# x, the memory and the constant columns arrive transposed; the head splits them k tile by k tile

## The chip, the cores and the metric

The kernel runs on one core of one Trainium2 chip. The metric is the time of the whole kernel on the device in microseconds (us). TensorE, VectorE, ScalarE, GpSimd and SyncE are written PE, DVE, ACT, POOL and SP, as in the profile; PEld is PE's weight load. SP issues nearly all transfers (DMAs) here, in the order of its program. Layout work that the host does on the inputs before the launch is not part of the time.

## The reference

One block of a network on 512 tokens of 1,024 numbers: a mixer (an HGRN2 recurrence and an mLSTM, four heads each), attention to a memory of 256 rows, and a convolutional feed-forward, each with a residual and a layer norm.

```python
proj = x @ w_in + b_in                  # (512,1024) @ (1024,4104)
hq, hf, hi, hg, mq, mk, mv, mo, mi, mf = split(proj)   # 8 x 512 columns, then 4 + 4 gate columns
log_f = log(lb + (1 - lb) * sigmoid(hf))
o_hg = head_rms_norm(hgrn2(silu(hq), (1 - lb) * sigmoid(-hf), hi, log_f)) * silu(hg)
qk = silu(causal_dwconv(concat(mq, mk)))
h_ml = mlstm(q_ml, k_ml, mv, mi, log_sigmoid(mf))
o_ml = sigmoid(mo) * head_layer_norm(h_ml)
x = layer_norm(ALPHA * x + concat(o_hg, o_ml) @ w_out)
x = layer_norm(ALPHA * x + cross_attention(x, mem))    # k, v = mem @ wkv
x = layer_norm(ALPHA * x + conv_ffn(x))
```

## The kernel before

Every large product is made of three matmuls: an operand is split into a rounded high part and the rest (`wh`, `wl` for weights, `xTh`, `xTl` for x), and `mm3` (lines 155 to 158) adds high x high, high x low and low x high into one PSUM bank. The high part is an ACT copy, the low part a DVE subtraction: `split` (line 119) for weights, `split_evict` (line 244) for what comes out of PSUM. Weights come in pieces of 1 MB into three buffers called `raw` (`load_raw`, line 111), which are free again when both parts are made. `slab_units` loads 4 k tiles of 512 columns, `col_units` 8 k tiles of 256 columns; a k tile is 128 of the 1,024 numbers that a product sums over.

The head of the program (lines 92 to 108 and 261 to 303) makes the projection `HI`. x is loaded in four blocks of 128 tokens; `transpose_block` (line 249) turns each on PE (8 transposes of 128x128 into two banks, line 254) and splits it, and the matmuls of a block (`hi_mm`) follow as transposed blocks and weights are there. PE, ACT and DVE run in the written order in this part. Elsewhere the order on each engine is set by a scheduler from its own estimate of times, not by the source alone.

Behind the head, eight small DMAs fetch biases and convolution weights as rows (lines 308 to 316), three transposes and a DVE copy turn them into `cols`, one constant per partition and column (lines 322 to 326), and eight tiny operations make the bound `lb` of the forget gate. Two further loads (`hnw`, `mnw`) and the eight gate columns (`wif`) follow.

The gates of the mLSTM come next: 16 matmuls of `wif` with x (lines 362, 363), then a serial chain on DVE and ACT (lines 368 to 399: `z`, `e`, `bl`, `ae`, ...), and four small PE transposes of its result (line 404). In PE's order these four stand behind 78 matmuls of the projection `HF`, whose weights are the first two 1 MB pieces loaded with `col_units` (columns 0 to 255 and 256 to 511 of `HF`). In DVE's order the first operation of the gate chain (`z`, line 368) stands behind the low part of the second of these pieces (line 126).

Much later, between the mLSTM's convolutions and its heads, the memory is transposed by 16 PE transposes (line 581) into four banks and split into `mTh`, `mTl`.

Of the kernel before, what the change touches and what calls it, by code (L numbers as in the profile page):

```python
# [37 lines left out]
def hybrid_block_kernel(  # L38
    ctx: ExitStack,
    tc: tile.TileContext,  # L40
    x: bass.AP,
    mem: bass.AP,
    w_in: bass.AP,
    b_in: bass.AP,
    hg_lb_logits: bass.AP,
    hg_norm_w: bass.AP,
    ml_conv_w: bass.AP,
    ml_conv_b: bass.AP,
    ml_norm_w: bass.AP,
# [8 lines left out]
    ffn_w_up: bass.AP,  # L58
    ffn_conv_w: bass.AP,
    ffn_conv_b: bass.AP,  # L60
    ffn_w_down: bass.AP,
# [39 lines left out]
    w_in0 = w_in[0]  # L101
    xin = [X8(F32, "xin") for _ in range(2)]
    xblk = [xin[b // 2][:, (b % 2) * D:(b % 2 + 1) * D] for b in range(NB)]
    raw0 = wp.tile([P, 2048], F32, name="raw", tag="raw", bufs=3).rearrange("p (a c) -> p a c", a=4)
    for b in range(NB):
        nc.sync.dma_start(xblk[b], x[0, b * P:(b + 1) * P, :])
        if b < 2:
            nc.sync.dma_start(raw0[:, 2 * b:2 * b + 2, :], w_in0[2 * b * P:2 * (b + 1) * P, HI:HI + 512]
                              .rearrange("(k p) c -> p k c", p=P))

    def load_raw(src_list, shape):
        r = wp.tile([P, 2048], F32, name="raw", tag="raw", bufs=3)
# [15 lines left out]

    def slab_units(w, c0, nk, raw=None):

        k, per = 0, (2 if raw is not None else 4)
        while k < nk:
            n = min(4, nk - k)
            if k or raw is None:
                raw = load_raw(
                    lambda rv, k=k, n=n: [(rv[:, j:min(j + per, n), :],
                                           w[(k + j) * P:(k + min(j + per, n)) * P, c0:c0 + 512]
                                           .rearrange("(k p) c -> p k c", p=P)) for j in range(0, n, per)],
                    (4, 512))
# [20 lines left out]
    def slab(xh, xl, w, c0, nk, evict, blocks=NB, late=0, raw=None, mid=None, mid_k=4, halves=False):  # L160

# [14 lines left out]

        for u in slab_units(w, c0, nk, raw):
# [83 lines left out]
    def kslice(ts_, k, c0=0, n=S):  # L261
        o = (k % 4) * 512 + c0
        return ts_[k // 4][:, o:o + n]
# [13 lines left out]

    def hi_mm(b, u):
        k0, n, h, l = u
        for i in range(n):  # L280
            k = k0 + i
            mm3(ps[b], kslice(xTh, k, b * P, P), kslice(xTl, k, b * P, P), h[:, i, :], l[:, i, :],
                k == 0, k == KT - 1)

    units = slab_units(w_in0, HI, KT, raw0)
    with tc.manual_schedule(engines={mybir.EngineType.PE, mybir.EngineType.Activation, mybir.EngineType.DVE}):
        us = []
        tb = lambda b, **kw: transpose_block(xblk[b], b, xTh, xTl, **kw)
        tb(0, mid=lambda: us.append(next(units)))
        tb(1)  # L290
        hi_mm(0, us[0])
        us.append(next(units))
        hi_mm(1, us[0])
        tb(2)
        hi_mm(0, us[1])
        tb(3)
        hi_mm(1, us[1])
        for b in (2, 3):
            hi_mm(b, us[0])
            hi_mm(b, us[1])  # L300
        for u in units:
# [6 lines left out]
    rows = q1p.tile([P, 3, P], F32, name="rows")  # L308
    r2 = lambda ap: ap.rearrange("(r c) -> r c", c=P)
    nc.sync.dma_start(rows[0:32, 0, :], r2(b_in[0, 0:4096]))  # L310
    nc.sync.dma_start(rows[32:64, 0, :], ml_conv_w[0].rearrange("j (r c) -> (j r) c", c=P))
    nc.sync.dma_start(rows[64:72, 0, :], r2(ml_conv_b[0]))
    nc.sync.dma_start(rows[72:80, 0, :], hg_lb_logits.rearrange("j (r c) -> (j r) c", c=P))
    for j in range(4):
        src = ffn_conv_w[0, j] if j < 3 else ffn_conv_b[0]
        nc.sync.dma_start(rows[44 * (j % 2):44 * (j % 2) + 44, 1 + j // 2, :], r2(src))
# [5 lines left out]
    ps = mx_bank()  # L322
# [545 lines left out]
    def ln3_evict(b, ps, cs):  # L868
# [10 lines left out]

_INS = ['x', 'mem', 'w_in', 'b_in', 'hg_lb_logits', 'hg_norm_w', 'ml_conv_w', 'ml_conv_b', 'ml_norm_w',  # L880
        'w_out', 'ln1_g', 'ln1_b', 'ca_wq', 'ca_wkv', 'ca_wo', 'ln2_g', 'ln2_b',
        'ffn_w_up', 'ffn_conv_w', 'ffn_conv_b', 'ffn_w_down', 'ln3_g', 'ln3_b']

# [10 lines left out]


# [7 lines left out]
```

## Time and profile before

| | us |
|---|---|
| time, median of 3 runs | 829.31 |
| lowest and highest of the 3 | 828.69, 829.79 |
| time of the profiled execution | 829.24 |
| its span, first to last instruction | 827.5 |
| PE busy in the span | 809.6 |
| PE waits for another engine or a DMA, the five longest | 4.3, 2.4, 1.6, 1.1, 0.6 |

The span is 1.74 us shorter than the time of the same execution. Times in the rows are counted from the start of the span. In the chain of waits a row is a start, a length and what it was; "issue" is time in which nothing that the profile shows was waited for. In the table of stretches the columns are the stretch, its length, the busy time of five engines with the number of instructions, PE's granted clock as a share of full speed, the share of the 16 DMA engines that was busy, and GB/s.

### The profile page before, as it was taken

The page shows a single profiled execution, that of the slowest core. Times are in us where ns is not written, and L with a number is a line of the kernel's source. Part 1 is how long each engine was busy: PE and PEld are TensorE (multiplying, and loading weights), DVE is VectorE, ACT ScalarE, POOL GpSimd, SP SyncE. Part 2 cuts the span into 40 slices and gives each one's busy share as a digit, 9 for nine tenths or more (in the row PEclk, how much of TensorE's full clock was granted, in tenths as well). Part 3 has the DMA queues.
Part 4 walks back from the last instruction along what each step waited for, and adds up shares of the span by engine and source line. Part 5 has one row for each costly group of instructions (what it writes and reads, how often), then busy time and mean ns, then how long its engine had stood idle before and what let it go on. Part 6 is the DMA issues. An engine that isn't in the chain of part 4 may idle for free.

```text
span 827.5 us, 10149 instructions
## 1 busy us (share of the span) xinstructions
PE 809.6 (98%) x4051; PEld 682.2 (82%) x4051; DVE 504.4 (61%) x863; ACT 323.1 (39%) x443; POOL 31.6 (4%) x52
## 2 busy tenths in 40 slices
PE   8979999999999999999999999999999999999996
PEld 7868877778779888889988988888888888888885
DVE  4374378888878289338638685566665666224237
ACT  4169653344235215226512364444444444221110
POOL 1000100010120000000001000000000000000001
PEclk9999999999999999999999999999999999999998
DMA  7845534034426613431311533333333322242102
GB/s 250 188 93 134 133 65 102 12 91 102 143 74 220 239 51 137 168 102 52 102 51 51 154 104 101 102 102 102 102 103 101 91 83 83 75 153 70 59 0 102
DMA packets 85156, 87.88 MB, mean 106 GB/s; under 512 B 3184, under 2 KB 64880, under 8 KB 85108
## 3 DMA queue, kind: packets, MB, share of 16 engines
q1 hardware_dynamic: 84524, 84.58, 34.4%
q10 hardware_dynamic: 584, 2.64, 0.8%
q8 instruction: 32, 0.52, 0.3%
q14 instruction: 16, 0.13, 0.0%
HBM read 85.10 MB, written 2.12 MB: 105 GB/s over the span
## 4 chain that ended last, share of the span: by engine, by line
PE 88%; DVE 5%; DMA 3%; POOL 1%; ACT 1%; issue 1%; SPq 0%; DVEq 0%; ACTq 0%; POOLq 0%
PE mm L156 27%; PE mm L157 27%; PE mm L158 27%; DMA raw<-in_w_in_dram 3%; PE mx L254 1%; PE mx L605 1%; PE mx L617 1%; POOL ss L451 1%; DMA xin<-in_x_dram 1%; PE mx L492 1%; PE mx L493 1%; PE mx L156 0%; PE mx L158 0%; PE mx L157 0%; PE mx L445 0%
## 5 line engine op out<-in xcount | busy, mean ns | idle before, releaser
L126 DVE TENSOR_TENSOR wl<-raw,wh 128x1024 fp32r<-128x1024 f32 x138 | 168.1, 1223 | 233.1 <-ACT wh L125 232.1
L125 ACT CAST wh<-raw 128x1024 fp32r<-128x1024 f32 x138 | 145.2, 1055 | 247.9 <-PE mm L158 135.1
L156 PE MATMUL mm<-x2h,wh 128*128 128x512 f32 (+1 forms) x384 | 142.8, 372 | 0.0
L157 PE MATMUL mm<-x2l,wh 128*128 128x512 f32 (+1 forms) x384 | 142.6, 371 | 0.0
L158 PE MATMUL mm<-x2h,wl 128*128 128x512 f32 (+1 forms) x384 | 142.6, 371 | 0.0
L158 PEld LDWEIGHTS mm<-x2h,wl 128*128 128x128 f32 x384 | 72.4, 188 | 12.6
L157 PEld LDWEIGHTS mm<-x2l,wh 128*128 128x128 f32 x384 | 72.4, 188 | 12.5
L156 PEld LDWEIGHTS mm<-x2h,wh 128*128 128x128 f32 x384 | 72.4, 188 | 12.3
L157 PE MATMUL mm<-wl,hTh 128*128 128x512 f32 (+1 forms) x198 | 72.4, 366 | 0.0
L156 PE MATMUL mm<-wh,hTh 128*128 128x512 f32 (+1 forms) x198 | 72.4, 366 | 0.0
L826 DVE SCALAR_TENSOR_TENSOR fc<-mm,cols,fc 128x511 f32<-128x511 f32 x88 | 65.7, 747 | 1.5
L158 PE MATMUL mm<-wh,hTl 128*128 128x512 f32 (+1 forms) x180 | 65.8, 365 | 0.0
L156 PE MATMUL mm<-wh,xTh 128*128 128x512 f32 x128 | 52.1, 407 | 0.0
L158 PE MATMUL mm<-wh,xTl 128*128 128x512 f32 x128 | 51.6, 403 | 0.0
L157 PE MATMUL mm<-wl,xTh 128*128 128x512 f32 x128 | 51.4, 401 | 0.0
L156 PE MATMUL mm<-xTh,wh 128*128 128x512 f32 x128 | 51.2, 400 | 0.0
L157 PE MATMUL mm<-xTl,wh 128*128 128x512 f32 x128 | 51.0, 399 | 0.0
L158 PE MATMUL mm<-xTh,wl 128*128 128x512 f32 x128 | 50.9, 397 | 0.0
L156 PEld LDWEIGHTS mm<-wh,hTh 128*128 128x128 f32 x198 | 37.4, 189 | 6.1
L157 PEld LDWEIGHTS mm<-wl,hTh 128*128 128x128 f32 x198 | 37.4, 189 | 6.1
L158 PEld LDWEIGHTS mm<-wh,hTl 128*128 128x128 f32 x180 | 33.9, 189 | 5.5
L835 ACT CAST hTh<-fc 128x512 fp32r<-128x512 f32 x22 | 13.7, 622 | 55.8 <-DVE fc L834 55.8
(274 smaller groups left out, 1401.3 us busy)
## 6 DMA issues: line engine op xcount, KB each, us to landing
raw<-in_ffn_w_up_dram SPq DMA_DIRECT2D x44, 512.0 KB, 4.3
raw<-in_w_in_dram SPq DMA_DIRECT2D x14, 1024.0 KB, 8.1
raw<-in_ffn_w_down_dram SPq DMA_DIRECT2D x10, 1024.0 KB, 5.0
raw<-in_ca_wkv_dram SPq DMA_DIRECT2D x8, 1024.0 KB
raw<-in_w_out_dram SPq DMA_DIRECT2D x4, 1024.0 KB, 10.1
raw<-in_ca_wq_dram SPq DMA_DIRECT2D x4, 1024.0 KB, 7.2
raw<-in_ca_wo_dram SPq DMA_DIRECT2D x4, 1024.0 KB
wt<-scr ACTq DMA_DIRECT2D x4, 640.0 KB
```

The costliest lines, as they stand in the source:

```text
L125: A.copy(hv, src)
L126: V.tensor_sub(lv, src, f32(hv))
L156: T.matmul(ps, ah, bh, start=first, stop=False, skip_group_check=True)
L157: T.matmul(ps, ah, bl, start=False, stop=False, skip_group_check=True)
L158: T.matmul(ps, al, bh, start=False, stop=last, skip_group_check=True)
L254: T.transpose(ps[:, i * P:(i + 1) * P], src[:, k * P:(k + 1) * P], ident)
L451: G.tensor_tensor(out_, out_, neghalf[:, 0:n], op=OP.pow)
L492: T.matmul(at[:, s], ke[:, s], qe[:, s], start=True, stop=True, skip_group_check=True)
L493: T.matmul(at[0:CH, b * P + CH:(b + 1) * P], kxe[:, b, :], qbo[:, b, :], start=True, stop=True, skip_group_check=True)
L605: T.matmul(ps[:, 0:LEN[j]], kT_[:, j * P:(j + 1) * P], qT_[:, j * P:], start=True, stop=True)
L826: V.scalar_tensor_tensor(y[:, s:], ps[:, :S - s], col(FCW + (2 - s) * 44 + ft), y[:, s:], op0=OP.mult, op1=OP.add)
L835: A.copy(kslice(hTh, i), g)
```

## The change

The host hands over x transposed (`x_t`, 1024x512) beside x, the memory transposed (`mem_t`, 1024x256), and all constant columns as one array (`cols_in`, 128x256). The kernel drops the transposes of x, of the memory and of the constants. The head takes k tiles in five steps of 1, 1, 2, 2 and 2 (`HEAD`): each step loads its rows of the weights and of `x_t` into one `raw` buffer (two halves), makes the high part of the weights on ACT and the three other parts on DVE, and runs all four token blocks. x itself is still loaded later for the residual.

```diff
+HEAD = ((0, 1), (1, 1), (2, 2), (4, 2), (6, 2))
...
-    for b in range(NB):
-        nc.sync.dma_start(xblk[b], x[0, b * P:(b + 1) * P, :])
-        if b < 2:
-            nc.sync.dma_start(raw0[:, 2 * b:2 * b + 2, :], w_in0[2 * b * P:2 * (b + 1) * P, HI:HI + 512]
-                              .rearrange("(k p) c -> p k c", p=P))
+    xraw, raw0 = [], []
+    for j, (k0, n) in enumerate(HEAD):
+        xr = wp.tile([P, 2048], F32, name="raw", tag="raw", bufs=3)
+        xraw.append(xr.rearrange("p (a c) -> p a c", a=4))
+        raw0.append(xraw[-1][:, 2:4, :])
+        for dst, src in ((raw0[-1], w_in0[:, HI:HI + 512]), (xraw[-1], x_t)):
+            nc.sync.dma_start(dst[:, 0:n, :], src[k0 * P:(k0 + n) * P, :].rearrange("(k p) c -> p k c", p=P))
...
-        tb(0, mid=lambda: us.append(next(units)))
-        tb(1)
-        hi_mm(0, us[0])
...
+        for (k0, n), xr, wr in zip(HEAD, xraw, raw0):
+            h = wp.tile([P, 1024], F32R, name="wh", tag="wh", bufs=4).rearrange("p (a c) -> p a c", a=2)
+            l = wp.tile([P, 1024], F32R, name="wl", tag="wl", bufs=4).rearrange("p (a c) -> p a c", a=2)
+            xk = lambda ts_: ts_[k0 // 4].rearrange("p (a c) -> p a c", a=4)[:, k0 % 4:k0 % 4 + n, :]
+            A.copy(h[:, 0:n, :], wr[:, 0:n, :])
+            V.tensor_copy(xk(xTh), xr[:, 0:n, :])
+            V.tensor_sub(l[:, 0:n, :], wr[:, 0:n, :], f32(h[:, 0:n, :]))
+            V.tensor_sub(xk(xTl), xr[:, 0:n, :], f32(xk(xTh)))
             for b in range(NB):
-                hi_mm(b, u)
+                for i in range(n):
+                    k = k0 + i
+                    mm3(ps[b], kslice(xTh, k, b * P, P), kslice(xTl, k, b * P, P), h[:, i, :], l[:, i, :],
+                        k == 0, k == KT - 1)
...
-    nc.sync.dma_start(rows[0:32, 0, :], r2(b_in[0, 0:4096]))
...
-    T.transpose(ps[:, 0:80], rows[0:80, 0, :], ident[0:80, 0:80])
-    T.transpose(ps[:, 80:168], rows[0:88, 1, :], ident[0:88, 0:88])
-    T.transpose(ps[:, 168:256], rows[0:88, 2, :], ident[0:88, 0:88])
-    V.tensor_copy(cols, ps[:, 0:256])
+    nc.sync.dma_start(cols, cols_in)
...
-    memraw = load_raw(lambda rv: [(rv, mem[0].rearrange("(b p) c -> p b c", p=P))], (2, 1024))
+    memraw = load_raw(lambda rv: [(rv, mem_t.rearrange("(k p) c -> p k c", p=P))], (8, 256))
...
-                T.transpose(ps[:, i * 256 + b * P:i * 256 + (b + 1) * P], memraw[:, b, k * P:(k + 1) * P], ident)
-        s = slice(j * 512, (j + 1) * 512)
-        split_evict(ps, mTh[:, s], mTl[:, s])
+    for j in range(2):
+        s = slice(j * 4, (j + 1) * 4)
+        m8 = lambda t: t.rearrange("p (a c) -> p a c", a=8)[:, s, :]
+        A.copy(m8(mTh), memraw[:, s, :])
+        V.tensor_sub(m8(mTl), memraw[:, s, :], f32(m8(mTh)))
```

On SP, from the small loads behind the head to the first three 1 MB pieces of weights (`raw` with 128x8x256: the two of `HF` and the first of `HQ`), the order before is:

```order
L310 DMA rows<-in_b_in_dram 32x128
L311 DMA rows<-in_ml_conv_w_dram 32x128
L312 DMA rows<-in_ml_conv_b_dram 8x128
L313 DMA rows<-in_hg_lb_logits_dram 8x128
L316 DMA rows<-in_ffn_conv_w_dram 44x128 x3
L316 DMA rows<-in_ffn_conv_b_dram 44x128
L318 DMA hnw<-in_hg_norm_w_dram 128x512
L320 DMA mnw<-in_ml_norm_w_dram 128x512
L349 DMA wif<-in_w_in_dram 128x8x8
L358 DMA bif<-in_b_in_dram 4x1
L359 DMA bif<-in_b_in_dram 4x1
L116 DMA raw<-in_w_in_dram 128x8x256 x3
```

The same place on SP after the change, from the last two steps of the head on:

```order
L108 DMA raw<-in_w_in_dram 128x2x512
L108 DMA raw<-in_x_t_dram 128x2x512
L108 DMA raw<-in_w_in_dram 128x2x512
L108 DMA raw<-in_x_t_dram 128x2x512
L290 DMA binb<-in_b_in_dram 128x512
L294 DMA cols<-in_cols_in_dram 128x256
L296 DMA hnw<-in_hg_norm_w_dram 128x512
L298 DMA mnw<-in_ml_norm_w_dram 128x512
L321 DMA wif<-in_w_in_dram 128x8x8
L330 DMA bif<-in_b_in_dram 4x1
L331 DMA bif<-in_b_in_dram 4x1
L115 DMA raw<-in_w_in_dram 128x8x256 x3
```

The eight loads of rows are one load of columns, and the last pieces of the head stand where they stood. Each DMA signals on one of eight semaphores in turn, so a DMA waits for the one eight places ahead of it to land; the first piece of `HF` now waits in that way for the head's last piece of `x_t`, and for its buffer.

On DVE, from the eviction of `HI` (`hv`) to the first operation of the gate chain (`z`), before:

```order
L306 TENSOR_TENSOR hv<-mm,binb 128x512 x4
L326 COPY cols<-mx 128x256
L126 TENSOR_TENSOR wl<-raw,wh 128x1024
L329 TENSOR_SCALAR nbin<-cols 128x32
L333 TENSOR_TENSOR lbm<-cols 128x4
L335 TENSOR_TENSOR le<-cols,lbm 128x4
L336 TENSOR_TENSOR le<-cols,lbm 128x4
L339 TENSOR_TENSOR ls<-le 128x4
L341 RECIPROCAL lr<-ls 128x4
L344 TENSOR_TENSOR lb<-le,lr 128x4
L345 TENSOR_SCALAR oml<-lb 128x4
L368 TENSOR_SCALAR z<-mm,bif 4x512
```

On DVE at the same place after the change (the three `wl` are the two halves of the first piece of `HF` and the first half of the second):

```order
L313 RECIPROCAL lr<-ls 128x4
L328 TENSOR_TENSOR wh<-wif,wh 128x8x4
L316 TENSOR_TENSOR lb<-le,lr 128x4
L317 TENSOR_SCALAR oml<-lb 128x4
L125 TENSOR_TENSOR wl<-raw,wh 128x1024
L292 TENSOR_TENSOR hv<-mm,binb 128x512 x2
L125 TENSOR_TENSOR wl<-raw,wh 128x1024
L292 TENSOR_TENSOR hv<-mm,binb 128x512 x2
L125 TENSOR_TENSOR wl<-raw,wh 128x1024
L340 TENSOR_SCALAR z<-mm,bif 4x512
```

The tiny operations on `cols` moved ahead of the weights; `z` still stands behind the first half of the second piece of `HF`.

On PE, at the end of the last `mq` tile, before:

```order
L156 MATMUL mm<-xTh,wh 128x512
L157 MATMUL mm<-xTl,wh 128x512
L158 MATMUL mm<-xTh,wl 128x512
L581 MATMUL mm<-ident,raw 128x128 x16
L605 MATMUL mx<-u 128x512
```

and after:

```order
L154 MATMUL mm<-xTh,wh 128x512
L155 MATMUL mm<-xTl,wh 128x512
L156 MATMUL mm<-xTh,wl 128x512
L574 MATMUL mx<-u 128x512
L574 MATMUL mx<-u 128x384
```

The 16 transposes are gone and the mLSTM's first product follows at once. The ACT copies and DVE subtractions of the memory moved up, among the convolutions of the `mk` tiles.

## Rows read from the trace of the kernel before

**Rows 1.** Busy time of the engines, first part of the page.
```profile
PE 809.6 (98%) x4051; PEld 682.2 (82%) x4051; DVE 504.4 (61%) x863; ACT 323.1 (39%) x443; POOL 31.6 (4%) x52
```
**Rows 2.** What PE waited for: us in total, times, longest.
```profile
PE mx L404 <- ACT ae L399: 4.3, 1, 4.3
PE mx L445 <- DVE y L534: 2.4, 3, 1.1
PE mx L254 <- DMA xin<-in_x_dram: 1.6, 1, 1.6
```
**Rows 3.** Chain that ended last, 14 to 62 us: start, length, what.
```profile
18.76 20.91 DMA raw<-in_w_in_dram
...
39.77 1.06 ACT wh L125
...
40.86 1.23 DVE wl L126
...
43.60 0.76 DVE z L368
...
60.77 0.64 ACT ae L399
...
61.45 0.43 PE mx L404 x4
```
**Rows 4.** Timeline of PE: start, length, instruction [idle before].
```profile
35.54 0.48 PE L362 MATMUL mm<-xTh,wh 128*128 128x512 f32 x1
...
39.26 0.39 PE L156 MATMUL mm<-xTh,wh 128*128 128x512 f32 x1
...
56.72 0.39 PE L158 MATMUL mm<-xTh,wl 128*128 128x512 f32 x1
...
62.41 0.63 PE L157 MATMUL mm<-xTl,wh 128*128 128x512 f32 x1
...
65.31 0.40 PE L158 MATMUL mm<-xTh,wl 128*128 128x512 f32 x1
```
**Rows 5.** Table of stretches.
```profile
4.00:6.00 2.00, 1.95 (x10) 1.68 (x9) 0.00 (x0) 0.35 (x1) 0.00 (x0) 1.00 1.02 242
7.00:9.00 2.00, 0.92 (x5) 0.95 (x6) 1.38 (x2) 1.08 (x2) 0.00 (x0) 1.00 1.07 391
24.00:28.00 4.00, 4.00 (x19) 3.31 (x18) 0.32 (x2) 0.34 (x2) 0.29 (x1) 1.00 0.97 165
60.00:65.00 5.00, 3.55 (x12) 2.83 (x13) 1.21 (x3) 4.96 (x7) 0.00 (x0) 0.68 0.01 1
207.00:213.00 6.00, 6.00 (x29) 4.96 (x28) 6.00 (x11) 1.44 (x3) 0.00 (x0) 1.00 0.98 341
```
**Rows 6.** Chain that ended last, 0 to 20 us.
```profile
8.08 1.94 PE mx L254 x8
10.02 0.43 PE mm L156
...
14.22 0.23 PE mm L157
```
**Rows 7.** Timeline of SP: when DMAs were issued.
```profile
6.54 0.35 SPq L310 DMA_DIRECT2D rows<-in_b_in_dram  x1
...
15.70 0.29 SPq L316 DMA_DIRECT2D rows<-in_ffn_conv_b_dram  x1
...
18.25 6.03 SPq L116 DMA_DIRECT2D raw<-in_w_in_dram  x3
```
**Rows 8.** Timeline of ACT: the first piece of HF is there.
```profile
32.38 1.05 ACT L125 CAST wh<-raw 128x1024 fp32r<-128x1024 f32 x1 [7.71 <-DMA raw<-in_w_in_dram]
```
**Rows 9.** DVE's groups of instructions: count | busy, mean ns | idle before.
```profile
L246 DVE TENSOR_TENSOR xTl<-mx,xTh 128x512 fp32r<-128x512 f32 x8 | 5.3, 689 | 9.0 <-ACT xTh L245 9.0
L416 DVE TENSOR_SCALAR kin<-kin,oml 128x512 f32<-128x512 f32 x4 | 1.9, 480 | 3.1 <-ACT kin L415 3.1
```
**Rows 10.** Timeline of PE: the transposes of the memory.
```profile
203.74 1.91 PE L581 MATMUL mm<-ident,raw 128*128 128x128 f32 x16
```

More of the change, by code (lines that the diff above doesn't have):

```diff
@@ L41, in hybrid_block_kernel @@
     x: bass.AP,
-    mem: bass.AP,
+    x_t: bass.AP,
+    mem_t: bass.AP,
+    cols_in: bass.AP,
     w_in: bass.AP,
     b_in: bass.AP,
-    hg_lb_logits: bass.AP,
     hg_norm_w: bass.AP,
-    ml_conv_w: bass.AP,
-    ml_conv_b: bass.AP,
     ml_norm_w: bass.AP,
@@ L101, in hybrid_block_kernel @@
     w_in0 = w_in[0]
-    xin = [X8(F32, "xin") for _ in range(2)]
-    xblk = [xin[b // 2][:, (b % 2) * D:(b % 2 + 1) * D] for b in range(NB)]
-    raw0 = wp.tile([P, 2048], F32, name="raw", tag="raw", bufs=3).rearrange("p (a c) -> p a c", a=4)
-    for b in range(NB):
-        nc.sync.dma_start(xblk[b], x[0, b * P:(b + 1) * P, :])
-        if b < 2:
-            nc.sync.dma_start(raw0[:, 2 * b:2 * b + 2, :], w_in0[2 * b * P:2 * (b + 1) * P, HI:HI + 512]
-                              .rearrange("(k p) c -> p k c", p=P))
+    xraw, raw0 = [], []
[5 more added lines that the diff above has]
+            nc.sync.dma_start(dst[:, 0:n, :], src[k0 * P:(k0 + n) * P, :].rearrange("(k p) c -> p k c", p=P))
     def load_raw(src_list, shape):
@@ L127, in split, with slab_units @@
         return hv, lv
-    def slab_units(w, c0, nk, raw=None):
-        k, per = 0, (2 if raw is not None else 4)
+    def slab_units(w, c0, nk):
+        k, per = 0, 4
         while k < nk:
             n = min(4, nk - k)
[L134 to L139, printed above, removed]
+            raw = load_raw(
+                lambda rv, k=k, n=n: [(rv[:, j:min(j + per, n), :],
+                                       w[(k + j) * P:(k + min(j + per, n)) * P, c0:c0 + 512]
+                                       .rearrange("(k p) c -> p k c", p=P)) for j in range(0, n, per)],
+                (4, 512))
             for u in range(0, n, 2):
@@ L158, in mm3, with slab @@
         T.matmul(ps, al, bh, start=False, stop=last, skip_group_check=True)
-    def slab(xh, xl, w, c0, nk, evict, blocks=NB, late=0, raw=None, mid=None, mid_k=4, halves=False):
+    def slab(xh, xl, w, c0, nk, evict, blocks=NB, late=0, mid=None, mid_k=4, halves=False):
         ps = [mm_bank() for _ in range(blocks)]
@@ L175, in run @@
                     mm3(pb, xh(k, b), xl(k, b), h[:, i, cs], l[:, i, cs], k == 0, k == nk - 1)
-        for u in slab_units(w, c0, nk, raw):
+        for u in slab_units(w, c0, nk):
             k0, n, h, l = u
@@ L276, in hybrid_block_kernel @@
     ps = [mm_bank() for _ in range(NB)]
[L278 to L285, printed above, removed]
-    with tc.manual_schedule(engines={mybir.EngineType.PE, mybir.EngineType.Activation, mybir.EngineType.DVE}):
-        us = []
-        tb = lambda b, **kw: transpose_block(xblk[b], b, xTh, xTl, **kw)
-        tb(0, mid=lambda: us.append(next(units)))
-        tb(1)
-        hi_mm(0, us[0])
[L292 to L301, printed above, removed]
+    with tc.manual_schedule(engines={mybir.EngineType.PE, mybir.EngineType.Activation, mybir.EngineType.DVE}):
+        for (k0, n), xr, wr in zip(HEAD, xraw, raw0):
[6 more added lines that the diff above has]
+            V.tensor_sub(xk(xTl), xr[:, 0:n, :], f32(xk(xTh)))
             for b in range(NB):
-                hi_mm(b, u)
+                for i in range(n):
+                    k = k0 + i
+                    mm3(ps[b], kslice(xTh, k, b * P, P), kslice(xTl, k, b * P, P), h[:, i, :], l[:, i, :],
+                        k == 0, k == KT - 1)
     nc.sync.dma_start(binb, bcast(b_in[0, HI:HI + 512], 512))
@@ L306, in hybrid_block_kernel @@
         V.tensor_add(hv[:, b, :], ps[b], binb)
-    rows = q1p.tile([P, 3, P], F32, name="rows")
-    r2 = lambda ap: ap.rearrange("(r c) -> r c", c=P)
-    nc.sync.dma_start(rows[0:32, 0, :], r2(b_in[0, 0:4096]))
[L311 to L316, printed above, removed]
+    nc.sync.dma_start(cols, cols_in)
     hnw = q1p.tile([P, 512], F32, name="hnw")
@@ L877, in hybrid_block_kernel @@
     slab(tok(hTh), tok(hTl), ffn_w_down[0], 512, NPAIR, ln3_evict, late=4, halves=True)
-_INS = ['x', 'mem', 'w_in', 'b_in', 'hg_lb_logits', 'hg_norm_w', 'ml_conv_w', 'ml_conv_b', 'ml_norm_w',
+_INS = ['x', 'x_t', 'mem_t', 'cols_in', 'w_in', 'b_in', 'hg_norm_w', 'ml_norm_w',
         'w_out', 'ln1_g', 'ln1_b', 'ca_wq', 'ca_wkv', 'ca_wo', 'ln2_g', 'ln2_b',
-        'ffn_w_up', 'ffn_conv_w', 'ffn_conv_b', 'ffn_w_down', 'ln3_g', 'ln3_b']
+        'ffn_w_up', 'ffn_w_down', 'ln3_g', 'ln3_b']
 def build(shapes):
@@ L893, in build, with laid_out @@
     return nc
+def laid_out(inputs):
+    a = {n: np.asarray(v) for n, v in inputs.items()}
+    a["x_t"], a["mem_t"] = a["x"][0].T, a["mem"][0].T
+    rows = [a["b_in"][0, 0:4096], a["ml_conv_w"], a["ml_conv_b"], a["hg_lb_logits"],
+            a["ffn_conv_w"], a["ffn_conv_b"]]
+    a["cols_in"] = np.concatenate([r.reshape(-1, P) for r in rows]).T
+    return {n: np.ascontiguousarray(a[n]) for n in _INS}
 def kernel(**inputs):
     from concourse.bass_utils import run_bass_kernel_spmd as _run
-    arrays = {f"in_{n}_dram": np.ascontiguousarray(inputs[n]) for n in _INS}
+    arrays = {f"in_{n}_dram": v for n, v in laid_out(inputs).items()}
     nc = build({n: arrays[f"in_{n}_dram"].shape for n in _INS})
```

8 lines of the change are left out of this document (removed).

## The prediction

> **What bounds the kernel now.** I read the busy times first: PE is busy for 809.6 us of 827.5, so nearly everything that shortens PE's stream or one of its waits counts in full, and what the other engines save counts only where PE waits for them [rows 1]. The list of PE's waits comes next. The longest is a single one of 4.3 us: the four gate transposes (line 404) wait for the last ACT step of the gate chain (line 399). The first transposes of x wait 1.6 us for their data [rows 2].
>
> The chain of waits tells why the 4.3 us are there. The weights of the second piece of `HF` land at 39.67 (18.76 + 20.91). ACT copies (1.06), DVE subtracts (1.23), and eight tiny operations follow until `z` starts at 43.60; the gate chain runs to 61.41, and PE goes on at 61.45 [rows 3]. So from `z` to PE's restart it is 17.85 us. PE itself had begun the gate matmuls at 35.54 and the 78 matmuls of `HF` at 39.26, 0.227 us apart (77 steps to 56.72), and was through them at about 57.0 [rows 4]. The late end is that of the gate chain, and its start hangs on a transfer, not on PE.
>
> The wait has a second price. From 60 to 65 us the granted clock is 0.68 on average [rows 5], and single matmuls last 0.63 where they last 0.40 from 65.31 on [rows 4]: after standing still, PE runs at 1.2 GHz and then again at 2.4. Some 8 matmuls at 0.43 apart instead of 0.227 are 1.65 us. In the head the chain's pieces show the same two levels: 0.43 per matmul from 10.02, 0.23 from 14.22, about 6 us after PE has begun to work without a pause at 8.08 [rows 6].
>
> **The head.** The 32 transposes of x go. What is left on PE up to the gate matmuls is 96 matmuls. Before, the first two transfers (1 MB) had landed when SP went on at 6.54 [rows 7], and half of that, one block of x, allowed the first transposes at about 4.5. The new first step needs the same half megabyte (weights and x of one k tile), so its data are there at about 4.5. A DVE cast of 512 columns from SBUF has no row; the nearest are 0.480 for a scalar operation and 0.689 for a subtraction [rows 9], I take 0.5. First matmul at 5.0; the second and third each wait for one more DVE subtraction, so PE works without a pause from about 6.3, not from 8.08. If the clock rises as long after that as before, it does so at 12.2; then 15.7 matmuls are done and the other 80.3 take 18.2 us: end at 30.4. Bounds: a rise 3.9 us after the start (as from 61.45 to 65.31) gives 29.5, a rise at 14.0 as before gives 31.2. DVE does not hold this up: two k tiles cost it 1.0 + 2 x 1.22 = 3.4 us, PE 24 x 0.227 = 5.4 us. The tightest place is the third step, whose second megabyte lands at 9.2 to 10 at 391 GB/s [rows 5] and is split by 12.6 to 13.4; PE comes there at 14.1.
>
> The Trainium skill (DMA: Bandwidth & Descriptors, section Bandwidth) says that DMAs should be at least 1 MiB to reach three quarters of the peak, which speaks against steps of 256 KB. Here 512 KB transfers queued one behind the other ran at 391 GB/s [rows 5]; smaller pieces in the same queue are shown by no row.
>
> The 16 gate matmuls end at 30.4 + 3.65 = 34.05, where the trace has 39.26: PE is 5.2 us ahead. It is through the 78 `HF` matmuls at 34.05 + 17.7 = 51.8, if the first piece of `HF` is split by 34 (it was there at 32.38 before [rows 8] and comes earlier, below).
>
> **The loads behind the head.** The three transposes and the copy of `cols` (0.4 us each or less) are hidden or gone; one load replaces eight. What counts is SP's order. Each of the eight had to wait for an older transfer to land, the last was issued at 15.70, and the first piece of `HF` at 18.25 [rows 7]. Now it waits for the head's last x, the same 4 MB, which before had landed shortly before 15.70: I take 15.2. That is 3.05 us sooner. The second piece needs a buffer whose last use is DVE's fourth step, at about 16.7. In front of both stand `binb` and `cols`, 384 KB or about 1.0 us at 391 GB/s. With the queue's pace unchanged the second piece lands at 39.67 - 3.05 + 1.0 = 37.6, call it 37.5.
>
> The pace is the open cost. Over 24 to 28 us the engines were 97% busy and moved 165 GB/s; later, on `ca_wkv`, 341 [rows 5]. At 165 GB/s on average the two pieces (2.1 MB) take 12.7 us; that they took longer before must be engines that lag behind the others. Begun at about 18.5, behind `hnw`, `mnw` and `wif`, and with all engines even, they land at about 32. At 341 GB/s they would be there before 27. I take the middle between 32 and 37.5, that is 34.7: there is no longer a standstill of the queue behind the head, but nothing makes these reads fast.
>
> The Trainium skill (the same page, section Latency and other measured facts) reports that rows spaced at large powers of two read slowly and that a small pad does not help; its rows are much longer than the 16,416 bytes of `w_in`. By that rule the slow reads belong to `w_in` and stay, which is the first rival's time. The trace agrees in part: `ca_wkv`, spaced at exactly 8,192 bytes, is the fast one.
>
> **The gate chain.** The eight tiny operations now stand before the weights. With the second piece at 34.7, ACT starts at 34.8, DVE's subtraction ends at 37.1, `z` starts, and PE restarts at 37.1 + 17.85 = 54.95 instead of 61.45: 6.5 us. PE then waits 3.1 us. Whether the clock falls after a pause that is a quarter shorter no row shows; I take half of the 1.65 us as gained: 0.8.
>
> **The memory.** 16 transposes last 1.91 us on PE [rows 10], 1.75 without the overlap with the next matmul. PE waits for nothing there, before or after, so 1.75 is gained. ACT's copies and DVE's subtractions (as many columns as before) move up beside the `mk` tiles. ACT now waits for the memory's load with a copy of `yTh` and two evictions of `mk` behind it; the load was on its way some 6 us before that place, so I cost the wait at nothing, and at up to 1 us if it is late.
>
> **Sum.** 6.5 + 0.8 + 1.75 = 9.05 us, from the profiled execution's 829.24 (0.07 below the median of the runs): 820.2.
>
> **Rivals.**
> First, the reads keep their pace, with the same laggards: the second piece at 37.5, `z` at 39.9, PE's restart at 57.75. 3.7 + 1.75 = 5.45, and the slow stretch stays: 823.8. For it: every first stretch of a `w_in` load is slow. Against it: the standstill before these loads is gone.
>
> Second, the reads are quick and PE is the bound: once the piece lands before about 31.5, `z` starts when the gate matmuls are done, 34.2, the chain ends at 52.05, and PE has been there since 51.8. 9.4 + 1.65 + 1.75 = 12.8: 816.4. For it: the head's reads of the same weights run at 391 GB/s when x lies between them, and now nothing stops in between.
>
> Third, slower: `w_in` is read slowly throughout. Its pieces now come first, in small steps; at the 242 GB/s of 4 to 6 us [rows 5] the head's 4.2 MB end 5.1 us later than they did, and if both pieces of `HF` take the 14.1 us that the first took from issue (18.25 to 32.38), the second lands at 15.2 + 5.1 + 28.2 = 48.5. PE restarts at 68.75: 7.3 lost, 1.75 gained, 834.8. It decides from a landing after 44.7 on. Against it: reads between x's were fast from 7 us on.
>
> That the change does little is the case between the first and third: a landing at 41 to 44.
>
> **How the numbers follow.** The forecast (820.2, on its own 817.5 to 822.5) has 0.42, the first rival 0.26, the second 0.21, the third 0.06, and 0.05 lie at no change, within 0.2% or 1.7 us, which is about what this kernel's runs can tell apart. Faster is the sum of the first three: 0.89. The range that should hold the time 8 times in 10 reaches from below the second rival's 816.4, for a clock that rises early (0.9 us) and a little more, to above the first rival's 823.8 with a longer slow stretch and 1 us lost at the memory: 814.5 to 826.5.
>
> **What would show it.** In the changed profile: PE's first matmul of `HI` near 5 us and the last gate matmul near 34; the second piece of `HF` landing near 35; `z` about 2.4 us after it; one wait of PE before the gate transposes, of 2 to 4 us, and the granted clock after it; no transposes before the mLSTM's first product. I am wrong if the second piece lands before 31 or after 37, if PE starves between the five steps of the head, or if a new wait of PE appears beside the `mk` tiles or in the mLSTM's heads, where the order changed too.

## The result and the profile after

The changed kernel takes 819.93 us (median of four runs, 819.76 to 821.82); the kernel before, run beside it, 829.49 (828.69 to 829.79). The ratio is 0.9891, interval 0.9874 to 0.9908: faster by 9.6 us. The forecast was 820.2, with 814.5 to 826.5 as the range. The profiled execution took 819.77, 9.47 less than the profiled one of before; its span is 818.1, shorter by 9.4. A second set of runs, below, gives 8.3 us (ratio 0.9898).

Busy time of the engines after the change; it answers to [rows 1]:

```profile
PE 801.5 (98%) x4000; PEld 674.0 (82%) x4000; DVE 504.9 (62%) x863; ACT 318.8 (39%) x434; POOL 30.2 (4%) x52
```

What PE waited for (us in total, times, longest); it answers to [rows 2]:

```profile
PE mx L376 <- ACT ae L371: 3.5, 1, 3.5
PE mx L417 <- DVE y L506: 2.4, 3, 1.1
PE mx L210 <- DVE warm L207: 1.1, 1, 1.1
PE mm L154 <- DVE xTh L282: 0.8, 1, 0.8
PE mm L156 <- DVE xTl L284: 0.6, 1, 0.6
PE mm L155 <- DVE wl L283: 0.5, 1, 0.5
```

The gate transposes (now line 376) are still the longest wait, still on the last ACT step of the gate chain, for 3.5 us instead of 4.3. The 1.6 us for x are gone; three shorter waits inside the head have taken their place.

The chain that ended last (start, length, what); it answers to [rows 3]:

```profile
9.26 7.34 DMA binb<-in_b_in_dram
...
16.68 17.60 DMA raw<-in_w_in_dram
...
34.39 1.06 ACT wh L124
...
36.73 0.75 DVE z L340
...
53.89 0.64 ACT ae L371
...
54.57 0.43 PE mx L376 x4
```

It has the same shape as before. The second piece of `HF` lands at 34.28 (16.68 + 17.60), ACT and DVE split its first half, `z` starts at 36.73, and 17.84 us later PE goes on, at 54.57 instead of 61.45.

PE in the head, at the gate matmuls and around the pause (start, length, what, idle time before); it answers to [rows 4]:

```profile
5.24 0.47 PE L154 MATMUL mm<-wh,xTh 128*128 128x512 f32 x1 [0.77 <-DVE xTh L282]
...
6.69 0.40 PE L154 MATMUL mm<-wh,xTh 128*128 128x512 f32 x1
6.93 0.40 PE L155 MATMUL mm<-wl,xTh 128*128 128x512 f32 x1
...
12.45 0.50 PE L155 MATMUL mm<-wl,xTh 128*128 128x512 f32 x1 [0.54 <-DVE wl L283]
13.59 0.50 PE L156 MATMUL mm<-wh,xTl 128*128 128x512 f32 x1 [0.63 <-DVE xTl L284]
...
32.99 0.39 PE L335 MATMUL mm<-xTl,wh 128*128 128x512 f32 x1
...
50.67 0.39 PE L156 MATMUL mm<-xTh,wl 128*128 128x512 f32 x1
54.57 0.43 PE L376 MATMUL mx<-ident,ae 36*128 36x36 f32 x4 [3.52 <-ACT ae L371]
...
56.25 0.63 PE L156 MATMUL mm<-xTh,wl 128*128 128x512 f32 x1
...
59.62 0.40 PE L155 MATMUL mm<-xTl,wh 128*128 128x512 f32 x1
```

Two things are to be seen. From 6.7 us on the matmuls stand 0.23 apart, the pitch of the higher level, 2.4 GHz. In the head the level can be read off the pitch alone: the granted clock in the table of stretches is 1.00 there in both kernels, also where the matmuls of before were 0.43 apart [rows 6]:

```profile
10.00:14.00 4.00, 4.00 (x11) 3.12 (x10) 2.43 (x3) 1.53 (x2) 0.00 (x0) 1.00 1.04 407
```

And after the pause of 3.5 us the clock falls all the same, 1.6 us later, for about 3.4 us (56.2 to 59.6), as long as before.

Two stretches of the table (columns as in [rows 5]):

```profile
22.00:26.00 4.00, 4.00 (x20) 3.30 (x19) 0.00 (x0) 0.00 (x0) 0.00 (x0) 1.00 0.29 95
56.00:60.00 4.00, 4.00 (x12) 3.14 (x11) 2.33 (x4) 3.56 (x5) 0.00 (x0) 0.57 0.00 0
```

While the first piece of `HF` is awaited, the DMA engines are 29% busy and move 95 GB/s, less than the 165 of before over 24 to 28 us, when they were 97% busy [rows 5]. These are two kinds of slowness. Divided by 16 engines and their busy share, it is 20.5 GB/s for a busy engine here and 10.6 there (estimates from these rows): after the change an engine is not slow while it is busy, but idle for most of the time. What the engines wait for no row shows.

SP's issue of the pieces of `HF`, DVE's first step on x in the third step of the head, and the mLSTM's first product, where the 16 transposes stood [rows 7, 9, 10]:

```profile
16.05 5.00 SPq L115 DMA_DIRECT2D raw<-in_w_in_dram  x3
```
```profile
10.57 0.69 DVE L282 CAST xTh<-raw 128x1024 fp32r<-128x1024 f32 x1 [2.30 <-DMA raw<-in_x_t_dram]
```
```profile
196.84 2.10 PE L574 MATMUL mx<-u 128*128 128x512 f32 x6
```

Where the 9.4 us of the span come from is read at four places. PE's restart: 61.45 - 54.57 = 6.88. The end of the projections, where before the transposes begin: 203.74 - 196.84 = 6.90, so nothing was won or lost in between. The mLSTM's first product: 205.48 - 196.84 = 8.64, the transposes' 1.74. The last matmul: 819.99 - 810.75 = 9.24: another 0.6 us. That is a wait of 0.6 us which before followed the mLSTM's first products and which the list of waits after the change no longer has. Before:

```profile
PE mx L605 <- DVE wt L606: 0.6, 1, 0.6
```

### The profile page after: what moved, and what is told of

Its sections match the earlier page's. It is cut to its first block, busy times and chain, and to the rows that moved or that the text cites. A ratio compares the mean times of both kernels' runs of the same rounds, so it can differ in the third digit from the quotient of the medians.

```text
span 818.1 us, 10034 instructions
## 1 busy us (share of the span) xinstructions
PE 801.5 (98%) x4000; PEld 674.0 (82%) x4000; DVE 504.9 (62%) x863; ACT 318.8 (39%) x434; POOL 30.2 (4%) x52
## 3 DMA queue, kind: packets, MB, share of 16 engines
q1 hardware_dynamic: 85632, 84.58, 33.6%
## 4 chain that ended last, share of the span: by engine, by line
PE 88%; DVE 5%; DMA 4%; POOL 1%; issue 1%; ACT 0%; SPq 0%; DVEq 0%; ACTq 0%; POOLq 0%
PE mm L154 27%; PE mm L155 27%; PE mm L156 27%; DMA raw<-in_w_in_dram 3%; PE mx L574 1%; DMA binb<-in_b_in_dram 1%; PE mx L586 1%; PE mx L252 1%; PE mx L464 1%; POOL ss L423 1%; DMA raw<-in_x_t_dram 1%; PE mx L465 1%; PE mx L154 0%; DVE wl L125 0%; PE mx L156 0%
## 5 line engine op out<-in xcount | busy, mean ns | idle before, releaser
L125 DVE TENSOR_TENSOR wl<-raw,wh 128x1024 fp32r<-128x1024 f32 x134 | 163.2, 1221 | 230.3 <-ACT wh L124 229.7
L124 ACT CAST wh<-raw 128x1024 fp32r<-128x1024 f32 x134 | 140.7, 1052 | 242.8 <-PE mm L156 133.0
```

What stands on the lines that cost most here:

```text
L124: A.copy(hv, src)
L125: V.tensor_sub(lv, src, f32(hv))
```

## The experiments

Each kernel ran beside the kernel before, whose medians in the three sessions were 829.10, 828.83 and 828.95; ratios are to those. What is read from a profile is read from one execution.

The theory: the second piece of `HF` decides when `z` starts and so when PE goes on; the head on PE matters only up to that point. Rivals: PE's own head brings the gain; or the parts gain by something else.

**The memory alone.** The kernel before with the memory's lines of the change.

```diff
-    memraw = load_raw(lambda rv: [(rv, mem[0].rearrange("(b p) c -> p b c", p=P))], (2, 1024))
+    memraw = load_raw(lambda rv: [(rv, mem_t.rearrange("(k p) c -> p k c", p=P))], (8, 256))
...
```

> The kernel before with the transposed memory alone; the head and the constants are as before. Theory 1: the parts add up, and what the whole change gained beyond the head and the 16 transposes (about 0.7 us, after the transposes' place in the program) comes with the new order of the memory's work: 1.75 + 0.7, so 827.0 us. Rival: the 0.7 us come from the head or the constants: 1.75 alone, 827.7. Rival 2: the memory's load, late for the new place of the ACT copy, holds up two evictions: 828.7 and a new wait of PE beside the mk tiles. In all of them the gate transposes still wait 4.3 us, until 61.4.

Measured: 826.75, ratio 0.9976 (0.9965 to 0.9986), 2.4 us, nearest to theory 1. The interval, 1.2 to 2.9 us, holds the first rival's 1.75 too; what speaks for theory 1 is that the wait of 0.6 us for `wt` is gone from this profile. The profile holds a surprise, in the head, where nothing was edited. Timeline of PE and its longest wait:

```profile
9.65 0.39 PE L156 MATMUL mm<-wh,xTh 128*128 128x512 f32 x1
9.88 0.40 PE L157 MATMUL mm<-wl,xTh 128*128 128x512 f32 x1
...
32.71 0.48 PE L362 MATMUL mm<-xTh,wh 128*128 128x512 f32 x1
```
```profile
PE mx L404 <- ACT ae L399: 6.1, 1, 6.1
```

Here the old head's matmuls are 0.23 apart from the first on, where the shown execution of before had 0.43 up to 14 us [rows 6]. The gate matmuls began at 32.71 instead of 35.54, and PE waited longer in turn, 6.1 us instead of the 4.3 of all the expectations. It went on at 60.34.

**The head alone**, and the same kernel once more in a later session: the changed kernel with the 16 transposes and their four banks put back.

```diff
-    memraw = load_raw(lambda rv: [(rv, mem_t.rearrange("(k p) c -> p k c", p=P))], (8, 256))
+    memraw = load_raw(lambda rv: [(rv, mem[0].rearrange("(b p) c -> p b c", p=P))], (2, 1024))
...
```

> The changed kernel with the 16 transposes of the memory put back; the head and the constants stay changed. Theory 1: the head moves PE's restart from 61.45 to 54.6 and nothing else: 829.5 - 6.9 = 822.6 us, with the slow stretch behind the restart as long as before. Rival: the 0.7 us beyond the two known terms come with the head: 821.9. Rival 2: the two parts need each other (PE's order in the mLSTM heads changes with the memory's): more than 823.5.

> The changed kernel with the memory's transposes put back, once more. Theory (reads of w_in differ from one loading of a program to the next): the second piece of HF lands elsewhere than at 37.1, and the time follows it by 20.2 us and the slow stretch: between 822 and 825. Rival: it lands at 37 again and takes 825 again: then something in this program, with the same instructions up to there, slows the reads.

Measured: 825.12, ratio 0.9955 (0.9939 to 0.9972), and 824.71, 0.9949 (0.9936 to 0.9963). Rival 2 of the first expectation, it seemed: taking the memory's part out costs over 4 us. The profiles say how. The piece was copied from 37.16 in the first and from 36.04 in the second, so the landing is not fixed, but in both it is later than the 34.39 above. From the second:

```profile
36.04 2.00 ACT L124 CAST wh<-raw 128x1024 fp32r<-128x1024 f32 x2 [5.50 <-DMA raw<-in_w_in_dram]
```
```profile
56.23 0.64 PE L376 MATMUL mx<-ident,ae 36*128 36x36 f32 x4 [4.90 <-ACT ae L371]
```
```profile
48.00:75.00 27.00, 22.10 (x87) 17.68 (x85) 13.54 (x26) 22.14 (x25) 0.00 (x0) 0.87 0.46 107
```

PE's restart is 0.8 us later than in the changed kernel's second profile, below (56.23 against 55.42), and behind the longer pause (4.9 us) the granted clock of the same 27 us is 0.87 instead of 0.94, which costs (0.94 - 0.87) x 27 = 1.9 us. With 2.5 us for the memory that is 5.2; the spans differ by 4.7. Why the piece is a little later in this program stays open: its instructions up to there are the same. Four profiles with the memory transposed (the changed kernel's two and two below) copy the piece at 34.39 to 35.22, the two with the transposes later. The second run lands elsewhere than the first, as its theory had it, and takes the same time, as the rival had it; it decides nothing.

**The gate chain first.** DVE's low parts forced behind the gate chain's first operations.

```diff
-    V.tensor_tensor(e, e, z, op=OP.min)
+    z_done = V.tensor_tensor(e, e, z, op=OP.min)
...
-    V.tensor_tensor_scan(bl, one4, z, 0.0, op0=OP.mult, op1=OP.add)
+    bl_done = V.tensor_tensor_scan(bl, one4, z, 0.0, op0=OP.mult, op1=OP.add)
...
+    hf = col_units(w_in0, HF, 4)
+    for i in range(4):
+        with tc.issue_after(z_done.ins) if i == 2 else ExitStack():
+            _, h, l = next(hf)
...
+        with tc.issue_after(bl_done.ins) if i == 0 else ExitStack():
+            _, h, l = next(hq)
```

> The changed kernel, with two orders forced on DVE: the low part of the second piece of HF stands behind the first operations of the gate chain, and the low part of the first piece of HQ behind the scan. Theory (the landing of the second piece is what holds up z): z starts at about 34.1, right behind the evictions of HI and the gate matmuls, 2.6 us sooner; the chain ends at 51 to 52; PE, through with the HF matmuls at 51.1, waits 0 to 1 us, and its clock does not fall: 3 us from the wait and 1.7 from the clock, 815.2 us. Rival: the chain is as late for another reason (the DVE subtractions then stand inside it, ACT's table loads): the end moves by less than 1 us, 819 to 820. Rival 2: the low parts come too late for PE, a new wait beside the HF matmuls of 1 to 2 us: 817.

Measured: 820.52, ratio 0.9901 (0.9884 to 0.9918): no gain over the changed kernel. The time is the first rival's, but not for its reason: the chain was as early as the theory had it. `z` started at 34.02, PE reached the gate transposes at 50.87 without a wait and the clock stayed up; but then:

```profile
PE mx L470 <- DVE ee L448: 2.9, 1, 2.9
```
```profile
94.60 0.72 ACT L576 ACTIVATE wt<-wt,aec 128x512 f32<-128x512 f32 x1 [10.93 <-DMA wt<-scr]
```
```profile
112.00:121.00 9.00, 9.00 (x34) 7.34 (x34) 5.22 (x9) 0.71 (x2) 0.00 (x0) 0.51 0.44 118
```
```profile
82.62 11.96 DMA wt<-scr
```

At the first HGRN head PE waits for DVE, and then the clock is at half over these 9 us. The new order had moved more than the gate chain: ACT stood 10.9 us on a load of `wt` with two weight copies behind it. The chain that ended last runs through this load (the last row), on to ACT's copies and over DVE to PE's wait.

**The gate chain first, and the products for `hgate` later.** As above, and:

```diff
-        V.tensor_mul(u, u, hnw)
-        V.tensor_mul(hgate[:, b, :], hgate[:, b, :], u)
+        hg_rest.append((b, u))
...
+        ee_done = V.tensor_mul(eo(e3)[:, :, 0, :], eo(e3)[:, :, 0, :], eo(q)[:, :, 0, :])
+        with tc.issue_after(ee_done.ins):
+            while hg_rest:
+                b, u = hg_rest.pop(0)
+                V.tensor_mul(u, u, hnw)
+                V.tensor_mul(hgate[:, b, :], hgate[:, b, :], u)
```

> The kernel with the gate chain first, and on top of it DVE's eight products for hgate stand behind the first HGRN head's products instead of among them. Theory (what the earlier gate chain gained was lost at the first HGRN head, where PE waited 2.9 us and its clock fell for 10 us): the head's products are ready 2 to 3 us sooner, PE waits 0 to 1 us, its clock stays up: 2 us of waiting and up to 4.8 of clock less, 814 to 817. Rival: DVE is only late at the next place, the evictions or the second head: 819 to 820.5.

Measured: 817.17 (815.8 to 818.7), ratio 0.9859 (0.9843 to 0.9875). The wait is 1.9 us now, and in the profiled execution (815.8, the fastest of four) the clock did not fall. The forecast, 814 to 817 with a wait of 0 to 1, was a little too good. So what the earlier chain had won was taken back at that place, and part of it comes out when the place is eased.

```profile
PE mx L476 <- DVE ee L449: 1.9, 1, 1.9
```

**The old head without its pause.** The kernel before with matmuls on zeros where PE waited 1.6 us for x.

```diff
         tb(0, mid=lambda: us.append(next(units)))
+        for _ in range(3):
+            T.matmul(wps[:, 0:P], warm, warm, start=True, stop=True)
         tb(1)
```

> The kernel before, with three more matmuls on zeros between the first two blocks of x, so that PE does not stand still for 1.6 us there. Theory on the clock: what keeps it at 1.2 GHz up to 14.0 us in the kernel before is that pause; without it the matmuls are 0.23 apart from about 7 us on, as in the changed kernel, and the gate matmuls end 1 to 3 us sooner than 39.3. Rival: it is the transposes that hold the clock down: 0.43 apart until 14 again. Theory on the time: PE's head decides nothing, since the second piece of HF lands at 39.7 as before and PE only waits longer for the gate chain: 829.4 us, within 0.5; if PE's head decides, 827 to 828.

Measured: 830.07, ratio 1.0017 (1.0007 to 1.0027): not faster, rather 1 us slower. The gate matmuls began at 32.72 with the clock up, as forecast, but the kernel with the memory alone shows the same head without the filler, so this run cannot tell what lifts the clock. What it does tell, beside the shown execution of before: 2.8 us less on PE's head gain nothing. PE came to the gate transposes sooner, waited 6.6 us and went on at 60.85 (61.45 before), and then the clock fell for longer:

```profile
60.85 0.64 PE L406 MATMUL mx<-ident,ae 36*128 36x36 f32 x4 [6.56 <-ACT ae L401]
```
```profile
48.00:75.00 27.00, 20.44 (x81) 16.34 (x80) 14.72 (x28) 22.50 (x26) 0.00 (x0) 0.81 0.49 86
```

That does not explain the 1 us, because the shown execution of before is not the usual one. Its mean granted clock over the span is 0.995; in 35 of the 41 executions of the kernel before that ran beside these experiments it is 0.991 to 0.993, and in this kernel's ten 0.992 to 0.994. The three other profiles with the old head (the memory alone, this one, and before with `HF` apart, below) begin the gate matmuls at 32.7 to 33.1, not at 35.5. So most executions of before, too, are likely to have had the quick head and the long pause; where the 1 us comes from stays open.

**The changed kernel again**, beside the next ones.

> The changed kernel once more, for runs beside those of the next kernels, and a second profile. Theory 1 (the landing of the second piece of HF varies by itself from execution to execution): it lands anywhere from 34 to 37.5, the gate transposes come 20.2 us behind that, and the pause before them is 3.5 to 6 us. Rival: this kernel lands it at 34.3 each time, and the 37.1 seen with the memory's transposes put back comes from that edit. Time by both: 819.8 to 821.8, so that the change is worth 8 to 9.5 us.

Measured: 820.57, ratio 0.9898 (0.9883 to 0.9913). The piece was copied from 35.22, 0.8 later than in the first profile, and PE waited 4.0 us:

```profile
55.42 0.44 PE L376 MATMUL mx<-ident,ae 36*128 36x36 f32 x4 [4.00 <-ACT ae L371]
```

The landing does vary, but not as far as 37.1, so neither theory nor rival is decided. In the head this execution has the pitch of 0.43 until 9.0 us (0.23 from 6.7 in the first), and its gate matmuls end 0.4 us later, at 33.6. Against the kernel before of its session the change is worth 8.3 us.

**The constants as before.** Eight loads of rows, transposes and copy put back.

```diff
-    nc.sync.dma_start(cols, cols_in)
+    nc.sync.dma_start(rows[0:32, 0, :], r2(b_in[0, 0:4096]))
...
+    T.transpose(ps[:, 0:80], rows[0:80, 0, :], ident[0:80, 0:80])
...
+    V.tensor_copy(cols, ps[:, 0:256])
...
```

> The changed kernel with the constants loaded as before: eight loads of rows, three transposes, one copy. Theory (the eight loads held up HF's pieces on SP): the second piece lands 2 to 3 us later, at 36.5 to 38, and the end moves with it: 822.5. Rival: the eight loads wait for nothing any more, since the head's transfers are issued early, and cost only the three transposes (0.5 us): 820.5.

Measured: 824.03, ratio 0.9945 (0.9932 to 0.9957): 3.5 us slower than the run above, more than the theory had. SP comes to the first piece of `HF` at 19.08 instead of 16.43, 2.7 us later (3.05 in the prediction), and the second is copied from 36.69, 1.5 us later:

```profile
19.08 18.30 SPq L119 DMA_DIRECT2D raw<-in_w_in_dram  x4
```

PE goes on at 56.43, 1.0 us later than in the run above, after a pause of 5.3 us, and the clock of 48 to 75 us falls to 0.87, which costs 1.9. So of the 3.5 us the smaller part is the landing, the larger the clock, and some 0.6 are not accounted for.

**HF's weights from an array of their own**, with rows 4,096 bytes apart.

```diff
+    a["w_qf"] = a["w_in"][0][:, 0:1024]
...
-    for i, h, l in col_units(w_in0, HF, 4):
+    for i, h, l in col_units(w_qf, HF, 4):
```

> The changed kernel, with the weights of HF read from an array of their own, whose rows are 4,096 bytes apart (in w_in: 16,416); sizes, places and number of the transfers are the same. Theory (the distance of w_in's rows makes the reads slow): the two pieces land by 23 and 27 instead of 28.2 and 34.3; z starts at 34.1, held by the gate matmuls and the evictions of HI; PE restarts at 52, waits 1 us and keeps its clock up to there; the first HGRN head then takes part of it back, as where z was put first: 816 to 819. Rival 1 (the slow start belongs to the queue after the small loads, or to three pieces at once): landings within 1.5 us of 28.2 and 34.3, 820. Rival 2: the landing is early and the time is still 820, all of it being taken back at the HGRN heads.

Measured: 814.85 (814.46 to 815.23), ratio 0.9830 (0.9817 to 0.9844): 5.7 us faster than the changed kernel beside it, and the best of all that were run, with one other. The two pieces land at 25.8 and 28.5, not at 23 and 27, and still in time. Table, ACT, DVE, and wait of PE:

```profile
22.00:26.00 4.00, 4.00 (x19) 3.31 (x18) 0.65 (x5) 0.52 (x3) 0.00 (x0) 1.00 1.01 333
48.00:75.00 27.00, 26.79 (x121) 21.89 (x120) 11.89 (x18) 25.35 (x28) 0.29 (x1) 1.00 0.49 137
```
```profile
25.82 2.00 ACT L125 CAST wh<-raw 128x1024 fp32r<-128x1024 f32 x2 [2.42 <-PE mm L157]
```
```profile
33.47 0.74 DVE L341 TENSOR_SCALAR z<-mm,bif 4x512 f32<-4x512 f32 x1 [0.68 <-PE mm L336]
```
```profile
51.32 0.43 PE L377 MATMUL mx<-ident,ae 36*128 36x36 f32 x4 [0.21 <-ACT ae L372]
```

In the same four microseconds the engines move 333 GB/s instead of 95 (98 in the profile of the run beside it). ACT no longer waits for the piece but for a buffer, `z` waits for the gate matmuls, PE for 0.2 us, and the clock does not fall behind the pause. PE goes on 4.1 us sooner than in the run beside it (51.32, 55.42), and the clock gives (1.00 - 0.94) x 27 = 1.6: together the 5.7. The forecast, 816 to 819, was too high: it had reckoned with a loss at the first HGRN head, but nothing was taken back there; the order on the engines is that of the changed kernel. That is the prediction's second rival (816.4), reached by another edit.

**The same edit in the kernel before, with the memory's transposes, and with a finer head.**

```diff
-            V.tensor_copy(xk(xTh), xr[:, 0:n, :])
-            V.tensor_sub(l[:, 0:n, :], wr[:, 0:n, :], f32(h[:, 0:n, :]))
...
+            for i in range(n):
+                k, s = k0 + i, slice(i, i + 1)
+                V.tensor_copy(xk(xTh)[:, s, :], xr[:, s, :])
+                V.tensor_sub(l[:, s, :], wr[:, s, :], f32(h[:, s, :]))
...
+                for b in range(NB):
```

> The kernel before with HF's weights alone read from an array with rows 4,096 bytes apart. Theory (there too the landing of the second piece is what bounds, and behind it comes PE): the pieces land 7 to 10 us sooner; z starts when the gate matmuls and DVE's small operations are through, at 37 to 39.5; the chain ends at 55 to 57.3, where PE is through with the HF matmuls at 54 to 57: a pause under 2 us, no fall of the clock. 4 to 6.4 us and 1.65 us: 821 to 823.5. What the head is worth is then the rest to the changed kernel with the same edit (814.9), less the memory's part: 4 to 6 us. Rival: the old head's eight loads and x hold up HF's loads so that the pitch hardly counts: 827 or more.

> The changed kernel with HF's weights from the array of their own, and the 16 transposes of the memory put back. Theory (the parts add up where no late transfer lies between them): the memory's part costs its 1.75 us and up to 0.6 for the other order behind it, 816.6 to 817.2, and the landings, z and PE's restart stay as without the transposes, 51.3. Rival: the 5 us by which the kernel with the head alone was slower belong to the memory's part in some other way: 819 to 820.

> The kernel with HF's weights apart, and DVE and PE going k tile by k tile through the head also in the steps of two k tiles. Theory (with the pieces early, PE's head sets when z starts): PE's 1 us of waiting in the third step goes, the gate matmuls end and z starts 1 us sooner, PE restarts at 50.3, 813.9. Rival: the two evictions and four low parts in front of z on DVE set its start now, and the 1 us is lost again: 814.9.

Measured, in this order: 823.14, ratio 0.9926 (0.9913 to 0.9939); 817.42, 0.9860 (0.9847 to 0.9874); 814.63, 0.9830 (0.9815 to 0.9844). With `HF` apart, the memory is worth 817.42 - 814.85 = 2.6 us, about the 2.4 that it gave by itself in the kernel before, and no longer the 4 to 5 of the late landing. Head and constants are worth the rest, 823.14 - 817.42 = 5.7; as a remainder that tests nothing. In the kernel before, the first piece came 3.6 us sooner than in the shown profile (28.75, 32.38), not 7 to 10, and the forecast of the time held. The finer head is the rival's: the gate matmuls began at 28.25 instead of 29.64, but `z` starts where it did, right behind a low part that stands before it on DVE:

```profile
32.14 1.22 DVE L126 TENSOR_TENSOR wl<-raw,wh 128x1024 fp32r<-128x1024 f32 x1
33.39 0.74 DVE L341 TENSOR_SCALAR z<-mm,bif 4x512 f32<-4x512 f32 x1
```

The profiles side by side (us, one execution each; clock: mean granted clock from 48 to 75 us; with `HF` apart the copy waits for a buffer, so its start is not the landing):

| kernel | second piece copied from | PE's pause | clock |
|---|---|---|---|
| before | 39.77 | 4.3 | 0.94 |
| memory alone | 38.66 | 6.1 | 0.87 |
| old head without its pause | 39.19 | 6.6 | 0.81 |
| head alone | 37.16, 36.04 | 6.0, 4.9 | 0.87, 0.87 |
| constants as before | 36.69 | 5.3 | 0.87 |
| changed | 34.39, 35.22 | 3.5, 4.0 | 0.94, 0.94 |
| gate chain first | 34.83 | none | 1.00, then 0.51 from 112 to 121 |
| gate chain first, `hgate` later | 34.97 | none | 1.00 |
| before, HF apart | 33.07 | 0.8 | 1.00 |
| HF apart, finer head | 29.06 | 1.5 | 0.94 |
| HF apart, memory's transposes | 29.96 | 0.2 | 1.00 |
| HF apart | 29.88 | 0.2 | 1.00 |

## Why the prediction was right

**The bound.** It named the landing of the second piece as what holds the end up, and that was right: with `HF` apart the landing came 6.7 us sooner (28.5, 35.2), and the kernel gained 5.7. In the changed kernel's two profiles and the two of the head alone, where the copy of the piece starts anywhere from 34.39 to 37.16, PE goes on 20.2 us behind it each time. Where PE's head alone was shorter (the memory alone, the filler), PE waited longer. From `z` to the restart it forecast 17.85 us and 17.84 were measured.

**The landing.** 34.7 was forecast, 34.28 measured. But the value was a middle between two paces, not a mechanism, and that it came so close is luck. (The 32 in it is 18.5 + 12.7 = 31.2, rounded up.) The pace did not become even: over 22 to 26 us it was slower than before. The landing came because the pieces were issued sooner (16.05; forecast 15.2) and because the pace rose later: 234 and 257 GB/s over 26 to 30 and 30 to 34 us, where before it was 131 and 157. The slow start, of which the first rival spoke, stayed, with the engines 29% busy where they had been 97% busy [rows 5]; what makes the pace recover sooner was not found. Of the sooner issue a run shows the worth: with the constants as before the second piece came 1.5 us later and the kernel took 3.5 us more.

**The head.** Two steps were wrong and hid each other. The clock's rise was put at 12.2, worked out from the rise at 14 in one execution; by the pitch it was up from 6.7, in the changed kernel's second profile from 9.0, and the kernel with the memory alone shows that the old head, too, can have it up by 9.65. That rise was a trait of an execution, not of the kernel. The Trainium skill (TensorE: Matmul & The Clock Gate, Part 1) says that the number of slow matmuls at a kernel's start differs from run to run; these executions agree with that. And PE was said not to starve between the five steps: it did, for 1.2 us in the third. That was named as the tightest place, with x split by 12.6 to 13.4 (DVE's cast took 0.69 of the 1.0 us reckoned, but x was there only at 10.57); the last part was ready at 13.5, and PE, at the higher clock, was there at 11.7. Together the gate matmuls ended at 33.2 instead of 34.05. Neither mattered for the time, because PE waited anyway. That the errors cancel is luck too.

**The clock behind the pause.** 0.8 us were forecast as gained, half of the cost; between the two shown profiles nothing was. The table above shows why half was no good guess: pauses of 3.5 to 4.3 us cost the same, longer ones more, one of 1.5 as much and those of 0.2 and 0.8 nothing. But the shown execution of before has an unusually short pause. Over the runs the median of the mean granted clock rises from 0.992 (41 executions before) to 0.995 (8 of the changed kernel), which on 820 us is 2.5 us by estimate. So most executions are likely to gain clock, and to win less at PE's restart.

**The memory.** 1.75 us were forecast; the transposes gave 1.74, and 0.6 more came from the wait behind the mLSTM's first products. "PE waits for nothing there, before or after" was the step that failed; 2.4 and 2.6 us were measured for the part in two ways.

**The sum.** Forecast 6.5 + 0.8 + 1.75 = 9.05; measured between the two shown profiles 6.88 + 0.0 + 1.74 + 0.6, and 0.2 behind the last matmul, 9.4. The 0.8 that failed and the 0.4 + 0.6 that were not counted nearly cancel.

**The order as a cure.** In the experiments the same reasoning failed once: 815.2 was forecast for the gate chain first, 820.52 measured. The sum stopped at the removed wait and did not ask what PE, 5 us ahead, would meet at the HGRN head.

## What to carry to other kernels

Follow the longest wait of the busiest engine back to its origin; if that is a transfer, shortening the engine's own work in front of it only lengthens the wait, and in these profiles a longer pause was followed by a longer stretch at the low clock. So a pause of a few microseconds on PE has two prices, and the second did not shrink in step: it was the same for pauses of 1.5 to 4.3 us and gone at 0.8. Before the order on an engine is changed to remove a wait, look for the next place where the engine that gets ahead will wait; and before that, ask whether the late transfer itself can be made faster. And before a sum is built on one profile, ask whether that execution is a usual one: here the mean granted clock of the runs said that it was not.

## What the runs showed that was not expected

Reading 1 MB of weights out of `w_in` (rows 16,416 bytes apart) went at 95 GB/s over 4 us, with the engines 29% busy; the same transfers out of an array with rows 4,096 bytes apart went at 333, with the engines busy throughout (1.01), and the kernel gained 5.7 us. For a busy engine that is 20.5 and 20.6 GB/s (estimates from the two rows): in the changed kernel an engine is not slower while it reads, it is idle for most of the time. The Trainium skill (DMA: Bandwidth & Descriptors, Latency and other measured facts) warns of rows spaced at large powers of two; here the power of two is the fast one, at a spacing far below those it lists. `ca_wkv` (8,192 bytes, 341 GB/s [rows 5]), in which the prediction saw the rule agree in part, speaks against it as well. Whether the spacing or the place of the array in memory does it, and what the idle engines wait for, no run separated.

A pause of PE of 3.5 us was followed by 3.4 us at 1.2 GHz that began only 1.6 us after PE had gone on.
